# Gate parts of the modulation summed on VectorE, and a three-operation S5 scan step, in a two-layer diffusion trunk

## The chip, the core and the metric

The kernel runs on one NeuronCore of one Trainium2 chip. A core has TensorE (PE, matrix products), VectorE (DVE), ScalarE (ACT), GpSimd (POOL) and SyncE (SP), each with its own instruction queue that is worked off in order, and 16 DMA engines that bring data from HBM into the core's memory (SBUF). Products land in PSUM. The metric is the device time of one execution in microseconds, as a median over runs; a lower time is better.

## The reference

The kernel computes one inference step of two trunk layers for 128 context tokens and 128 latent tokens of width 2048. Cut to what matters here, a layer is:

```python
mod = c_silu @ w_mod[l] + b_mod[l]                      # 2048 x 6144, for the two conditions c_ctx and c
shift, scale, gate = jnp.split(mod, 3, axis=-1)
h = rms_norm(x, norm_w[l]) * (1 + scale) + shift
hg, at, s5_u, s5_g, merge = split_columns(h @ w_in[l])  # 2048 x 15872
o_hg, o_at = hgrn_branch(hg), attention(at)
u = s5_u.reshape(bsz, seq, 64, 16)                      # S5: 64 groups, 64 complex states each
s_t = abar * s_{t-1} + bbar @ u_t                       # forward, and backward over flipped tokens
y = gelu(re(c @ s) + d * s5_u)
o_s5 = y * sigmoid(y @ w_glu) * silu(s5_g)
merged = sum(sigmoid(merge_b) * (o_b @ w_br[b]) for b in (hg, at, s5))
x = x + gate * (merged @ w_out[l])
```

The modulation is a product of two vectors with a matrix of 2048 x 6144 per layer. The kernel cuts its 6144 columns into six parts of 1024: parts 0 to 3 hold shift and scale, parts 4 and 5 hold the gate, which is used only behind the product with `w_out`.

## The kernel before

Everything is in fp32. A large product goes through `gemm` (L160): its weights come in pieces of 512 KB (`raw`, L167, three buffers) through SP's queue; each piece holds two k-steps of 128 rows. Per k-step ACT rounds the weights to `wh` and DVE subtracts them to get the rest `wl` (L139), and PE makes three products (L178 to L180) for each of the two streams, in all six matmuls of 512 columns. `wh` and `wl` have four buffers each, so neither can be more than four k-steps ahead of PE.

A layer makes its products in this order: the columns of `w_in` for S5, attention and the recurrent branch, with attention, the recurrence (`hgrn_unit`) and the S5 branch worked in between; the output gates of two branches; then for each branch b the merge gates (`m0`, `m1`, `m2`) and the product with `w_br`; for the S5 branch the product with `w_glu` stands between the merge gates and `w_br`; last `w_out`.

The S5 branch is cut into four quarters per layer (`s5_quarter`, L785). A quarter forms its inputs, then runs 64 scan steps on DVE over the tile `Sb`, which holds the inputs and then the states of both directions; before, a step is four operations (L828, L830, L833, L834). When the scan is over, PE forms the output `yp` (L840, L847). `Sb`, and later `ghl` (GELU of the branch, the left side of the product with `w_glu`, L1036), lie in the one buffer of tag S16.

The modulation is made by `mod_part` (L245), one part of 1024 columns at a time. Before, PE multiplies 16 weight tiles of 128 x 1024 with the conditions as stationary side, each cut into four pieces of 256 columns that go to four column groups of the array (L274); then DVE adds the bias (L279). For parts 4 and 5, POOL stores the result in HBM, from where it is read back, spread over all partitions (`gb`), behind `w_out`. Parts (0, 4) and (0, 5) of layer 0, the first four parts of layer 1, and parts (1, 4) and (1, 5) are "side work": a generator that `gemm` advances at a set rate (`MRATE`) from the second branch's merge gates on.

What sets the order: the code gives each instruction a priority (`P_SCAN`, `P_TOP` and others; a smaller one goes first), and a scheduler that plays through a time line puts each engine's instructions into one fixed order before the program runs. A change of cost in one place can thus move instructions anywhere.

The lines that the prediction's steps touch:

```python
w = self.t(tag if isinstance(tag, str) else tag[i], "wm", (128, n * 1024))
nc.sync.dma_start(w, io["w_mod"][l, part, k][:, i * 1024:(i + n) * 1024])
...
wl = self.wp.tile([128, 512], F32R, tag="wl", name=self.nm("wl"))
...
Sb = self.t("S16", "Sb", (128, 2, 2, 8, 2, W))
...
ghl = self.t("S16", "ghl", (128, 2, 8, 256), F32R)
```

Of the kernel before, what the change touches and what calls it, by code (L numbers as in the profile page):

```python
# [15 lines left out]
ALU = mybir.AluOpType  # L16
# [12 lines left out]
MB = 2  # L29
# [19 lines left out]
P_TOP = 1_000_000  # L49
# [3 lines left out]
P_MIX = 0  # L53
# [4 lines left out]
def view(t, off, dims):  # L58
    return bass.AP(t.tensor, t.offset + off, [list(t.ap[0])] + [list(d) for d in dims])


class Builder:
    def __init__(self, tc, ctx, io):
        self.tc, self.nc, self.io = tc, tc.nc, io
        self.seq = 0
        pool = lambda name, bufs, **kw: ctx.enter_context(tc.tile_pool(name=name, bufs=bufs, **kw))
        self.cp = pool("const", 1)
        self.wp = pool("weights", 4)
        self.sb = pool("sb", 1)
        self.bufs = dict(H8=4, Z8=2, Bl=1, CC=1, S16=1, uT=1, U2=1, ys=1, q4=2, kv=2,  # L70
                         mo=1, st=10, k2=6, k4=3, gt=4, sm=18, s5i=4, p=4, sb=1, sc=1, s5t=1)
        self.pg = pool("pg", 4, space=PSUM)
        self.pm = pool("pm", 2, space=PSUM)
        self.pb = pool("pb", 2, space=PSUM)
        self.dr = pool("scratch", 1, space=DRAM)
        self.uid = 0
# [32 lines left out]
    def ts(self, n, shape, dt=F32):  # L109
        return self.t("sm", n, shape, dt)  # L110
# [99 lines left out]
    def setup(self):  # L210
        nc, io = self.nc, self.io
        mf = self.t("ys", "masks", (128, 7, 128))
        nc.gpsimd.dma_start(mf, io["masks"])
        self.msk = self.const("msk", (128, 7, 128), U8)
        nc.vector.tensor_copy(self.msk, mf)
        self.eye32 = self.const("eye32", (128, 32), src=io["eye32"])
        self.cosT = self.const("cosT", (128, 128), src=io["rope"][0])
        self.sinT = self.const("sinT", (128, 128), src=io["rope"][1])
        self.s5d = self.const("s5d", (128, L, 8), src=io["s5_d"])
        self.gate_d = self.dr.tile([L, 2, D], F32, name="gate_d")  # L220
        self.x_d = self.dr.tile([2, T, D], F32, name="x_d")
# [20 lines left out]
        nc.vector.tensor_scalar(self.oml, self.lb, -1.0, 1.0, ALU.mult, ALU.add)  # L242


    def mod_part(self, l, part, prio, tags, plan):  # L245


# [2 lines left out]
        nc, io = self.nc, self.io  # L250
        with self.prio(prio):
            bm = self.t("mo", "bm", (128, 352))[:, 0:256]
            src = io["b_mod"][l, part]
            nc.gpsimd.dma_start(bm, bass.AP(src.tensor, src.offset, [[256, 4], [0, 32], [1, 256]]))
        kb = 0
        for bank, run, burst in plan:
            ps = None
            for k0 in range(kb, kb + run, burst):
                ws = []
                for k in range(k0, k0 + burst):  # L260
                    with self.prio(P_TOP):
                        tag, n = next(tags)
                        for i in range(0, 2, n):
                            w = self.t(tag if isinstance(tag, str) else tag[i], "wm", (128, n * 1024))
                            nc.sync.dma_start(w, io["w_mod"][l, part, k][:, i * 1024:(i + n) * 1024])
                            ws += [w[:, j * 1024:(j + 1) * 1024] for j in range(n)]
# [375 lines left out]
    def s5_params(self, l):  # L642
# [50 lines left out]

        cmul(a2r, a2i, abr, abi, abr, abi)
        cmul(acr, aci, abr, abi, cr, ci)
        sc = self.const(f"s5sc{l}", (128, 384))
        o = lambda off, ds: view(sc, off, ds)
        for qd in range(4):
            for d in range(2):
                i = qd * 2 + d  # L700
                pm = lambda c: view(c, d * 32 + qd * 8, [[1, 2], [2, 2], [4, 2]])
                for ri in range(2):
                    nc.vector.tensor_copy(o(i * 16 + ri * 8, [[4, 2], [2, 2], [1, 2]]), pm(a2r))
                    for st in range(2):
                        ts(o(128 + i * 32 + ri * 16 + st, [[8, 2], [4, 2], [2, 2]]), pm(a2i), 2.0 * ri - 1.0, None, ALU.mult)
        self.s5sc[l] = sc

    def s5_input(self, l, qd, Bl, C, Sb):
# [76 lines left out]
    def s5_quarter(self, l, hh, qh, uT, U2, ys):  # L785
# [3 lines left out]
        W = NP + 1  # L789
# [32 lines left out]
        sc = self.s5sc[l]  # L822
        with self.prio(P_SCAN):
            for i in range(NP):
                p0 = self.t("p", "p0", (128, 2, 32))
                p1 = self.t("p", "p1", (128, 2, 32))
                ds = DD + NP - 2 * i
                tt(p0.rearrange("p d (j s) -> p d j s", s=2), view(sc, qd * 32, [[16, 2], [1, 16], [0, 2]]),  # L828
                   view(Sb, i, [[ds, 2], [2 * W, 16], [W, 2]]), ALU.mult)
                tt(p1, view(sc, 128 + qd * 64, [[32, 2], [16, 2], [1, 16]]),  # L830
                   view(Sb, i + RI, [[ds, 2], [-RI, 2], [W, 16]]), ALU.mult)
                cur = view(Sb, i + 1, [[ds - 2, 2], [W, 32]])
                tt(p0, p0, p1, ALU.add)  # L833
                tt(cur, cur, p0, ALU.add)  # L834
        with self.prio(P_S5):
            yp = self.psb("yp", (128, 2, 2, 2, NP))
            for k in range(2):
# [371 lines left out]
```

## Time and profile before

| | us |
|---|---|
| median of 3 runs | 2330.3 (2329.36 to 2330.72) |
| the profiled execution, its own time | 2331.88 |
| its span, first to last instruction | 2330.1 |
| PE busy in the span | 2257.9 (97%) |
| DVE busy | 1798.2 (77%) |
| ACT busy | 1180.8 (51%) |
| POOL busy | 133.9 (6%) |
| mean granted TensorE clock | 0.994 of full speed |

Busy time is the union of an engine's instructions. PE, PEld (PE's weight loads), DVE, ACT and POOL are the engines; SPq is SyncE's queue of DMA issues. "L139" is line 139 of the kernel before. The chain of work that ended last is followed back from the last instruction, at each step to what released it. A name such as `wl<-raw,wh` tells what an instruction writes and reads, without the numbers of the buffers.

### The profile page before, as it was taken

To read this page: it belongs to the slowest core of one execution; us is meant where nothing else is said; L and a number is where in the kernel's file an instruction comes from. 1 tells how busy PE (TensorE), PEld (TensorE's weight loads), DVE (VectorE), ACT (ScalarE), POOL (GpSimd) and SP (SyncE) were. 2 spreads that over 40 slices of the span, in tenths; PEclk is the share of its full clock that TensorE was granted. 3 is DMA by queue.
4 is the path that set the end of the run, shared out by engine and by line. 5 is a ranking of instruction groups with operands and counts; after the bars stand their busy time and mean duration, and the time that the engine had idled before them with its cause. 6 is when DMAs were issued, how large, how long until landed. Compare 5 with 4: busy or idle time off the path is not lost.

```text
span 2330.1 us, 38207 instructions
## 1 busy us (share of the span) xinstructions
PE 2257.9 (97%) x13192; PEld 1812.2 (78%) x13192; DVE 1798.2 (77%) x4835; ACT 1180.8 (51%) x2061; POOL 133.9 (6%) x244
## 2 busy tenths in 40 slices
PE   4999999999999999999998999999999999999997
PEld 2777877888887776887777888888878877887886
DVE  5856899799879868865565798899959968956555
ACT  3536645555554343544446565555564544454454
POOL 2000000100000100000010001000010010000000
PEclk9999999999999999999999999999999999999999
DMA  8994554355557878677874554454545677656765
GB/s 313 342 341 142 165 172 137 110 162 184 178 165 258 295 267 298 220 251 265 305 231 138 163 174 153 132 160 155 188 155 190 194 245 240 198 179 219 240 202 181
DMA packets 131490, 483.85 MB, mean 208 GB/s; under 512 B 17200, under 2 KB 17808, under 8 KB 126944
## 3 DMA queue, kind: packets, MB, share of 16 engines
q1 hardware_dynamic: 120528, 454.09, 58.2%
q0 software_dynamic: 9472, 23.97, 3.3%
q10 hardware_dynamic: 1296, 3.36, 0.4%
q8 instruction: 103, 1.69, 0.3%
q14 instruction: 91, 0.75, 0.1%
HBM read 474.36 MB, written 6.98 MB: 207 GB/s over the span
## 4 chain that ended last, share of the span: by engine, by line
PE 82%; DVE 8%; DMA 7%; issue 2%; ACT 1%; SPq 0%; POOL 0%; DVEq 0%; ACTq 0%; POOLq 0%
PE g L178 23%; PE g L180 23%; PE g L179 22%; DMA raw<-w_in 3%; DVE wl L139 3%; PE mod L274 3%; PE bu L816 3%; PE lv L432 2%; DMA raw<-w_br 2%; DMA wm<-w_mod 2%; PE tr L134 2%; PE yp L847 1%; DVE p L830 1%; DVE Sb L834 1%; ACT wh L138 1%
## 5 line engine op out<-in xcount | busy, mean ns | idle before, releaser
L138 ACT CAST wh<-raw 128x512 fp32r<-128x512 f32 x1344 | 819.4, 622 | 925.0 <-PE g L179 459.8
L139 DVE TENSOR_TENSOR wl<-raw,wh 128x512 fp32r<-128x512 f32 x1344 | 915.5, 689 | 368.5 <-ACT wh L138 319.1
L178 PE MATMUL g<-wh,hl 128*128 128x512 f32 x1984 | 785.1, 396 | 6.4 <-ACT wh L138 2.7
L179 PE MATMUL g<-wh,hh 128*128 128x512 f32 x1984 | 777.9, 392 | 0.0
L180 PE MATMUL g<-wl,hh 128*128 128x512 f32 x1984 | 700.9, 398 | 0.4 <-DVE wl L139 0.3
L178 PEld LDWEIGHTS g<-wh,hl 128*128 128x128 f32 x1984 | 373.5, 188 | 99.4 <-ACT wh L138 8.2
L179 PEld LDWEIGHTS g<-wh,hh 128*128 128x128 f32 x1984 | 373.6, 188 | 75.7 <-issue 0.2
L180 PEld LDWEIGHTS g<-wl,hh 128*128 128x128 f32 x1984 | 366.6, 189 | 82.5 <-DVE wl L139 5.8
L178 PE MATMUL g<-wh,ol 128*128 128x512 f32 x384 | 152.0, 396 | 2.5 <-ACT wh L138 2.3
L828 DVE TENSOR_TENSOR p<-s5sc,Sb 128x64 f32<-128x64 f32 x512 | 140.8, 275 | 14.9 <-ACT Sb L820 5.9
L179 PE MATMUL g<-wh,oh 128*128 128x512 f32 x384 | 149.9, 390 | 0.0
L834 DVE TENSOR_TENSOR Sb<-Sb,p 128x64 f32<-128x64 f32 x512 | 141.7, 277 | 8.9
L830 DVE TENSOR_TENSOR p<-s5sc,Sb 128x64 f32<-128x64 f32 x512 | 139.2, 272 | 0.0
L180 PE MATMUL g<-wl,oh 128*128 128x512 f32 x384 | 132.0, 393 | 0.8 <-DVE wl L139 0.8
L274 PE MATMUL mod<-wm,cs 128*32 128x256 f32 x1536 | 104.5, 404 | 26.6 <-DMA wm<-w_mod 20.1
L833 DVE TENSOR_TENSOR p<-p,p 128x64 f32<-128x64 f32 x512 | 113.6, 222 | 6.1
L274 PEld LDWEIGHTS mod<-wm,cs 128*32 128x32 f32 x1536 | 44.7, 113 | 77.1 <-DMA wm<-w_mod 24.1
L179 PE MATMUL g<-wh,mt 128*128 128x512 f32 x256 | 99.8, 390 | 0.0
L178 PE MATMUL g<-wh,mt 128*128 128x512 f32 x256 | 99.7, 389 | 0.0
L178 PEld LDWEIGHTS g<-wh,ol 128*128 128x128 f32 x384 | 72.1, 188 | 20.3 <-ACT wh L138 4.6
L180 PEld LDWEIGHTS g<-wl,oh 128*128 128x128 f32 x384 | 71.5, 188 | 17.6 <-DVE wl L139 2.4
L180 PE MATMUL g<-wl,mt 128*128 128x512 f32 x256 | 83.5, 393 | 1.7 <-DVE wl L139 1.7
(315 smaller groups left out, 2116.8 us busy)
## 6 DMA issues: line engine op xcount, KB each, us to landing
raw<-w_in SPq DMA_DIRECT2D x496, 512.0 KB, 3.8
wm<-w_mod SPq DMA_DIRECT2D x130, 512.0 KB, 7.2
raw<-w_br SPq DMA_DIRECT2D x96, 512.0 KB, 4.2
raw<-w_out SPq DMA_DIRECT2D x64, 512.0 KB, 4.3
wm<-w_mod SPq DMA_DIRECT2D x31, 1024.0 KB, 7.4
raw<-w_glu SPq DMA_DIRECT2D x16, 512.0 KB, 3.9
gb<-gate_d POOLq DMA_DIRECT2D x16, 256.0 KB, 6.0
x<-x ACTq DMA_DIRECT2D x2, 1024.0 KB, 14.0
```

Source lines behind the costliest of these rows:

```text
L134: nc.tensor.transpose(ps[:, k], src[:, k * 128:(k + 1) * 128], self.ident)
L138: self.nc.scalar.copy(hi, src)
L139: self.nc.vector.tensor_sub(lo, src, hi.bitcast(F32))
L178: nc.tensor.matmul(ps[s], lo(k)[:, sl], wh, start=(k == 0), stop=False)
L179: nc.tensor.matmul(ps[s], hi(k)[:, sl], wh, start=False, stop=False)
L180: nc.tensor.matmul(ps[s], hi(k)[:, sl], wl, start=False, stop=(k == nk - 1))
L274: nc.tensor.matmul(ps[32 * i:32 * i + 32, 0:256], self.cT[:, 2 * k:2 * k + 32], ws[k - 2 * k0][:, i * 256:i * 256 + 256], start=(k0 == kb ...
L816: nc.tensor.matmul(pps[x][:, j2, k], Bl[pr, d, ri, k, j2, :], U2[pr, j2, 2 * qh + k].rearrange("p s t -> p (s t)"), start=True, stop=True, ...
L828: tt(p0.rearrange("p d (j s) -> p d j s", s=2), view(sc, qd * 32, [[16, 2], [1, 16], [0, 2]]), view(Sb, i, [[ds, 2], [2 * W, 16], [W, 2]]) ...
L830: tt(p1, view(sc, 128 + qd * 64, [[32, 2], [16, 2], [1, 16]]), view(Sb, i + RI, [[ds, 2], [-RI, 2], [W, 16]]), ALU.mult)
L833: tt(p0, p0, p1, ALU.add)
L834: tt(cur, cur, p0, ALU.add)
```

## The change

The gate parts of both layers, (0, 4), (0, 5), (1, 4) and (1, 5), no longer go through PE's products with the condition. DVE keeps two running sums `acc` of 128 x 1024, one for each condition: for each of the 16 weight tiles and each condition one operation multiplies the tile with the condition's column (a scalar per partition) and adds it. At the end PE sums each `acc` over its partitions with a stationary tile of zeros and one column of ones, 8 matmuls of 256 columns per part. Loading is put into a function of its own, `mod_load`, whose priority, buffers and order are those of before.

In the S5 scan, the two products of a step become one of 128 elements (own part and crossed part, with a table `sc` in a new layout), then come one addition that reads the crossed half with real and imaginary part exchanged, and the update: three operations for four. Tag `p` has three buffers of twice the size; tag `va` is new; GpSimd's DMA scratch is set to 4096 bytes.

```diff
+VPARTS = {(0, 4), (0, 5), (1, 4), (1, 5)}
...
-                         mo=1, st=10, k2=6, k4=3, gt=4, sm=18, s5i=4, p=4, sb=1, sc=1, s5t=1)
+        self.bufs = dict(H8=4, Z8=2, Bl=1, CC=1, S16=1, va=2, uT=1, U2=1, ys=1, q4=2, kv=2,
+                         mo=1, st=10, k2=6, k4=3, gt=4, sm=18, s5i=4, p=3, sb=1, sc=1, s5t=1)
...
+        self.ones = self.const("ones", (128, 2, 32))
+        nc.gpsimd.memset(self.ones, 0.0)
+        for s in range(2):
+            nc.gpsimd.memset(self.ones[:, s, s:s + 1], 1.0)
...
+        if (l, part) in VPARTS:
+            acc = [self.t("va", "acc", (128, 1024)) for _ in range(2)]
+            for k0 in range(8):
+                ws = self.mod_load(l, part, k0, tags)
+                with self.prio(prio):
+                    for j, w in enumerate(ws):
+                        for s in range(2):
+                            c = self.cT[:, 4 * k0 + 2 * j + s:4 * k0 + 2 * j + s + 1]
+                            if k0 + j == 0:
+                                nc.vector.tensor_scalar(acc[s], w, c, None, ALU.mult)
+                            else:
+                                nc.vector.scalar_tensor_tensor(acc[s], w, c, acc[s], ALU.mult, ALU.add)
+                    if k0 == 7:
+                        ps = self.psm("mod", (128, 512))
+                        for i in range(4):
+                            for s in range(2):
+                                with self.prio(P_MIX if i + s else prio):
+                                    nc.tensor.matmul(ps[32 * i:32 * i + 32, 0:256], self.ones[:, s],
+                                                     acc[s][:, i * 256:i * 256 + 256], start=(s == 0), stop=(s == 1),
+                                                     tile_position=(0, 32 * i))
+                        nc.vector.tensor_add(bm, bm, ps[:, 0:256])
+                if k0 % MB == MB - 1 and k0 < 7:
+                    yield True
+            plan = ()
...
-        sc = self.const(f"s5sc{l}", (128, 384))
+        sc = self.const(f"s5sc{l}", (128, 512))
...
-                    nc.vector.tensor_copy(o(i * 16 + ri * 8, [[4, 2], [2, 2], [1, 2]]), pm(a2r))
                     for st in range(2):
-                        ts(o(128 + i * 32 + ri * 16 + st, [[8, 2], [4, 2], [2, 2]]), pm(a2i), 2.0 * ri - 1.0, None, ALU.mult)
+                        at = qd * 128 + d * 32 + ri * 16 + st
+                        nc.vector.tensor_copy(o(at, [[8, 2], [4, 2], [2, 2]]), pm(a2r))
+                        ts(o(at + 64, [[8, 2], [4, 2], [2, 2]]), pm(a2i), 1.0 - 2.0 * ri, None, ALU.mult)
...
-                p0 = self.t("p", "p0", (128, 2, 32))
-                p1 = self.t("p", "p1", (128, 2, 32))
+                p = self.t("p", "p", (128, 2, 2, 32))
                 ds = DD + NP - 2 * i
-                tt(p0.rearrange("p d (j s) -> p d j s", s=2), view(sc, qd * 32, [[16, 2], [1, 16], [0, 2]]),
-                   view(Sb, i, [[ds, 2], [2 * W, 16], [W, 2]]), ALU.mult)
-                tt(p1, view(sc, 128 + qd * 64, [[32, 2], [16, 2], [1, 16]]),
-                   view(Sb, i + RI, [[ds, 2], [-RI, 2], [W, 16]]), ALU.mult)
+                tt(p, view(sc, qd * 128, [[64, 2], [32, 2], [1, 32]]), view(Sb, i, [[0, 2], [ds, 2], [W, 32]]), ALU.mult)
                 cur = view(Sb, i + 1, [[ds - 2, 2], [W, 32]])
-                tt(p0, p0, p1, ALU.add)
-                tt(cur, cur, p0, ALU.add)
+                own = p[:, 0]
+                tt(own, own, view(p, 80, [[32, 2], [-16, 2], [1, 16]]), ALU.add)
+                tt(cur, cur, own, ALU.add)
...
-    nc = bacc.Bacc("TRN2", target_bir_lowering=False, num_devices=1)
+    nc = bacc.Bacc("TRN2", target_bir_lowering=False, num_devices=1, dynamic_dma_scratch_size=4096)
```

The scheduler's order is another one in many places. Three of them follow. The line numbers in an order are those of its own kernel: L139 before is L140 after, L178 to L180 are L179 to L181, and L828 to L834 have become L862, L865 and L866.

The first place is DVE in layer 0, ahead of the product with `w_glu`, at the end of the scan of the last quarter. `wl_10655` is the subtraction of k-step 511, `wl_10745` of 516; `Sb` holds the states, `ghl` is the left side of the product with `w_glu`, whose own weights are k-steps 528 to 543. Before:

```order
L834 TENSOR_TENSOR Sb_5242<-Sb_5242,p_1317_5766 128x2x32
L828 TENSOR_TENSOR p_1319_5772<-s5sc_341,Sb_5242 128x64
L830 TENSOR_TENSOR p_1320_5773<-s5sc_341,Sb_5242 128x64
L139 TENSOR_TENSOR wl_10655<-raw_10642,wh_10654 128x512
L833 TENSOR_TENSOR p_1319_5772<-p_1319_5772,p_1320_5773 128x64
L834 TENSOR_TENSOR Sb_5242<-Sb_5242,p_1319_5772 128x2x32
L139 TENSOR_TENSOR wl_10701<-raw_10698,wh_10700 128x512
...
L139 TENSOR_TENSOR wl_10733<-raw_10720,wh_10732 128x512
L139 TENSOR_TENSOR ghl_10904<-ys_1847,ghl_10904 128x512 x3
L139 TENSOR_TENSOR wl_10745<-raw_10742,wh_10744 128x512
```

After, where `wl_10414` and `wl_10424` are k-steps 530 and 531 and `wl_10436` is 532:

```order
L140 TENSOR_TENSOR wl_10414<-raw_10411,wh_10413 128x512
L865 TENSOR_TENSOR p_5134<-p_5134 128x64
L866 TENSOR_TENSOR Sb_4894<-Sb_4894,p_5134 128x2x32
L140 TENSOR_TENSOR wl_10424<-raw_10411,wh_10423 128x512
L862 TENSOR_TENSOR p_5138<-s5sc_345,Sb_4894 128x128
L865 TENSOR_TENSOR p_5138<-p_5138 128x64
L866 TENSOR_TENSOR Sb_4894<-Sb_4894,p_5138 128x2x32
...
L862 TENSOR_TENSOR p_5298<-s5sc_345,Sb_4894 128x128
L865 TENSOR_TENSOR p_5298<-p_5298 128x64
L866 TENSOR_TENSOR Sb_4894<-Sb_4894,p_5298 128x2x32
L140 TENSOR_TENSOR ghl_10372<-ys_1883,ghl_10372 128x512 x4
L140 TENSOR_TENSOR wl_10436<-raw_10433,wh_10435 128x512
```

The scan's last step stood behind k-step 511 and now stands behind 531; 41 steps, each of the three operations, stand between `wl_10424` and `ghl_10372` with nothing else among them. In layer 1 the same pattern holds 12 steps, behind its k-step 1203.

The second place is PE in layer 0 where the branch's output `yp` is formed. `wl_10655` is again k-step 511 of before, `wh_10700` step 512. Before:

```order
L180 MATMUL g_10454<-wl_10655,hh_1764 128x512
L847 MATMUL yp_5778<-Sb_5242,C_5236 32x128 x8
L847 MATMUL yp_5778<-Sb_5242,CC_5319 32x128 x8
L840 MATMUL yp_5778<-uT_4597,CC_5319 128x128
...
L178 MATMUL g_10668<-wh_10700,hl_554 128x512
```

After, where `wl_10359` is k-step 527 and `wh_10391` is step 528, the first of the product with `w_glu`:

```order
L181 MATMUL g_10137<-wl_10359,hh_1800 128x512
L879 MATMUL yp_5302<-Sb_4894,C_4888 32x128 x8
L879 MATMUL yp_5302<-Sb_4894,CC_4971 32x128 x8
L872 MATMUL yp_5302<-uT_4377,CC_4971 128x128
...
L179 MATMUL g_10387<-wh_10391,ghl_10372 128x512
```

`yp`, which reads the whole scan, had 16 k-steps of other products behind it; now the product with `w_glu` follows at once.

The third place is a gate part in layer 0. Before, on PE, a burst of a part stands between two k-steps of the `w_in` and `w_br` products:

```order
L180 MATMUL g_8896<-wl_9002,oh_8655 128x512
L274 MATMUL mod_9113<-wm_9111,cs 32x256 x4
L274 MATMUL mod_9113<-wm_9109,cs 32x256 x4
L274 MATMUL mod_9113<-wm_9107,cs 32x256 x4
L274 MATMUL mod_9113<-wm_9105,cs 32x256 x4
L178 MATMUL g_9015<-wh_9019,hl_554 128x512
```

After, on DVE, the sums of a part stand among the subtractions `wl`, the merge of the branches and the scan:

```order
L282 SCALAR_TENSOR_TENSOR acc_8323<-wm_8333,cs,acc_8323 128x1024
L1014 TENSOR_TENSOR merged_7079<-mg_7262,g_7266 128x512
L140 TENSOR_TENSOR wl_7394<-raw_7381,wh_7393 128x512
L282 SCALAR_TENSOR_TENSOR acc_8324<-wm_8333,cs,acc_8324 128x1024
L866 TENSOR_TENSOR Sb_2493<-Sb_2493,p_2877 128x2x32
L140 TENSOR_TENSOR wl_7406<-raw_7403,wh_7405 128x512
L140 TENSOR_TENSOR wl_7416<-raw_7403,wh_7415 128x512
L282 SCALAR_TENSOR_TENSOR acc_8323<-wm_8335,cs,acc_8323 128x1024
```

16 bursts of 32 PE records each have gone from PE's order, and 128 operations on 1024 elements have come into DVE's; the scan of a quarter that runs beside them is spread over more k-steps.

## Rows read from the trace of the kernel before

**Rows 1.** The page: busy time and share of PE; the chain's shares by engine.

```profile
PE 2257.9 (97%) x13192; PEld 1812.2 (78%) x13192; DVE 1798.2 (77%) x4835; ACT 1180.8 (51%) x2061; POOL 133.9 (6%) x244
...
PE 82%; DVE 8%; DMA 7%; issue 2%; ACT 1%; SPq 0%; POOL 0%; DVEq 0%; ACTq 0%; POOLq 0%
```

**Rows 2.** Groups by line: line, engine, operation, tiles, shapes, count | busy us, mean ns | idle

```profile
L138 ACT CAST wh<-raw 128x512 fp32r<-128x512 f32 x1344 | 819.4, 622 | 925.0 <-PE g L179 459.8
L139 DVE TENSOR_TENSOR wl<-raw,wh 128x512 fp32r<-128x512 f32 x1344 | 915.5, 689 | 368.5 <-ACT wh L138 319.1
...
L179 PE MATMUL g<-wh,hh 128*128 128x512 f32 x1984 | 777.9, 392 | 0.0
```

**Rows 3.** Timeline of PE, two product rows six apart: start us, us, instruction

```profile
803.07 0.39 PE L178 MATMUL g<-wh,hl 128*128 128x512 f32 x1
...
804.42 0.39 PE L178 MATMUL g<-wh,hl 128*128 128x512 f32 x1
```

**Rows 4.** Timeline of DVE, operations on 512 and 1024 elements in a row

```profile
231.28 0.68 DVE L139 TENSOR_TENSOR wl<-raw,wh 128x512 fp32r<-128x512 f32 x1
231.88 1.22 DVE L504 TENSOR_TENSOR q<-q,qnorm 128x1024 f32<-128x1024 f32 x1
233.01 0.69 DVE L139 TENSOR_TENSOR wl<-raw,wh 128x512 fp32r<-128x512 f32 x1
```

**Rows 5.** Timeline of PE around gate bursts of 32 and of 8 records

```profile
807.60 0.39 PE L180 MATMUL g<-wl,hh 128*128 128x512 f32 x1
807.92 1.93 PE L274 MATMUL mod<-wm,cs 128*32 128x256 f32 x32
809.78 0.50 PE L178 MATMUL g<-wh,hl 128*128 128x512 f32 x1
...
815.94 0.64 PE L274 MATMUL mod<-wm,cs 128*32 128x256 f32 x8
```

**Rows 6.** Windows, line L274 alone: PE busy (records), PEld, clock, DMA, GB/s

```profile
725.00:823.00 98.00, 16.10 (x256) 7.21 (x256) 1.00 0.86 307
1860.00:2330.00 470.00, 15.68 (x256) 7.42 (x256) 0.99 0.65 214
```

**Rows 7.** Timeline of DVE, last scan operation of layer 0

```profile
963.32 0.28 DVE L834 TENSOR_TENSOR Sb<-Sb,p 128x64 f32<-128x64 f32 x1
```

**Rows 8.** Timeline of PE, first matmul with w_glu in layer 0

```profile
992.34 0.39 PE L178 MATMUL g<-wh,ghl 128*128 128x512 f32 x1
```

**Rows 9.** Timeline of DVE, a scan step with nothing between its operations

```profile
359.74 0.28 DVE L828 TENSOR_TENSOR p<-s5sc,Sb 128x64 f32<-128x64 f32 x1
359.93 0.27 DVE L830 TENSOR_TENSOR p<-s5sc,Sb 128x64 f32<-128x64 f32 x1
360.23 0.23 DVE L833 TENSOR_TENSOR p<-p,p 128x64 f32<-128x64 f32 x1
360.49 0.28 DVE L834 TENSOR_TENSOR Sb<-Sb,p 128x64 f32<-128x64 f32 x1
360.80 0.27 DVE L828 TENSOR_TENSOR p<-s5sc,Sb 128x64 f32<-128x64 f32 x1
```

**Rows 10.** Timeline of PE at the change of layers; idle time before in brackets

```profile
1227.09 1.08 PE L134 MATMUL tr<-ident,xn 128*128 128x128 f32 x4 [6.46 <-DVE xn L322]
1230.12 1.08 PE L134 MATMUL tr<-ident,xn 128*128 128x128 f32 x4 [1.95 <-DVE xn L322]
```

**Rows 11.** Windows there: PE, PEld, DVE, ACT, POOL busy, granted clock, DMA, GB/s

```profile
1230.00:1235.00 5.00, 4.88 (x13) 3.85 (x14) 1.78 (x3) 2.36 (x6) 0.00 (x0) 0.50 0.00 0
1235.00:1240.00 5.00, 4.83 (x24) 3.80 (x22) 3.32 (x8) 2.79 (x6) 0.00 (x0) 0.93 0.00 0
```

**Rows 12.** The page, DMA issues: KB each, median us from issue to landing

```profile
wm<-w_mod SPq DMA_DIRECT2D x130, 512.0 KB, 7.2
raw<-w_br SPq DMA_DIRECT2D x96, 512.0 KB, 4.2
...
gb<-gate_d POOLq DMA_DIRECT2D x16, 256.0 KB, 6.0
```

More of the change, by code (lines that the diff above doesn't have):

```diff
@@ L69, in __init__ @@
         self.sb = pool("sb", 1)
-        self.bufs = dict(H8=4, Z8=2, Bl=1, CC=1, S16=1, uT=1, U2=1, ys=1, q4=2, kv=2,
-                         mo=1, st=10, k2=6, k4=3, gt=4, sm=18, s5i=4, p=4, sb=1, sc=1, s5t=1)
+        self.bufs = dict(H8=4, Z8=2, Bl=1, CC=1, S16=1, va=2, uT=1, U2=1, ys=1, q4=2, kv=2,
+                         mo=1, st=10, k2=6, k4=3, gt=4, sm=18, s5i=4, p=3, sb=1, sc=1, s5t=1)
         self.pg = pool("pg", 4, space=PSUM)
@@ L242, in lower_bounds, with mod_load @@
         nc.vector.tensor_scalar(self.oml, self.lb, -1.0, 1.0, ALU.mult, ALU.add)
+    def mod_load(self, l, part, k, tags):
+        ws = []
+        with self.prio(P_TOP):
+            tag, n = next(tags)
+            for i in range(0, 2, n):
+                w = self.t(tag if isinstance(tag, str) else tag[i], "wm", (128, n * 1024))
+                self.nc.sync.dma_start(w, self.io["w_mod"][l, part, k][:, i * 1024:(i + n) * 1024])
+                ws += [w[:, j * 1024:(j + 1) * 1024] for j in range(n)]
+        return ws
     def mod_part(self, l, part, prio, tags, plan):
@@ L260, in mod_part @@
                 for k in range(k0, k0 + burst):
[L261 to L266, printed above, removed]
+                    ws += self.mod_load(l, part, k, tags)
                 with self.prio(prio):
@@ L699, in s5_params @@
             for d in range(2):
-                i = qd * 2 + d
                 pm = lambda c: view(c, d * 32 + qd * 8, [[1, 2], [2, 2], [4, 2]])
                 for ri in range(2):
-                    nc.vector.tensor_copy(o(i * 16 + ri * 8, [[4, 2], [2, 2], [1, 2]]), pm(a2r))
                     for st in range(2):
-                        ts(o(128 + i * 32 + ri * 16 + st, [[8, 2], [4, 2], [2, 2]]), pm(a2i), 2.0 * ri - 1.0, None, ALU.mult)
+                        at = qd * 128 + d * 32 + ri * 16 + st
+                        nc.vector.tensor_copy(o(at, [[8, 2], [4, 2], [2, 2]]), pm(a2r))
+                        ts(o(at + 64, [[8, 2], [4, 2], [2, 2]]), pm(a2i), 1.0 - 2.0 * ri, None, ALU.mult)
         self.s5sc[l] = sc
```

## The prediction, made blind

> **What bounds the kernel now.** The shares of busy time come first: TensorE (PE) has work in 97% of the span, VectorE (DVE) in 77%, and the chain that ended last runs over PE for 82% and over DVE for 8% [rows 1]. The reader is to see there that a removed matmul is worth its full time, and that DVE counts only where PE waits for it. The groups by line show what PE does: a k-step of every product is one cast on ScalarE (ACT, 622 ns), one subtraction on DVE (689 ns) and six matmuls of 512 columns [rows 2]. Six of them take 804.42 - 803.07 = 1.35 us [rows 3], so DVE spends 0.60 us (231.28 to 231.88) [rows 4] of every 1.35 us on the subtraction, and the rest is free for the scan, the gates and now the sums. The PE row idles 3% only; I therefore add up PE's work, then look for places where the new order makes PE wait. Numbers in steps below count the `wl` rows of DVE's order, from 0; a layer has 672 of them, and the product with w_glu is steps 528 to 543 of layer 0 and 1200 to 1215 in layer 1.
>
> **What goes from PE.** A gate part is four bursts of 32 records. Around one, the next product starts 809.78 - 807.60 = 2.18 us after the last, where 0.23 would be usual, so a burst costs 1.95 us [rows 5]. Layer 0 has 256 such records and the second layer's gates have 256 [rows 6], that is 16 bursts: -31.2 us.
>
> **What comes to PE.** Each of four parts ends in 8 matmuls of 256 columns, 16 records. Four records on four column groups take (1.93 - 0.64) / 6 = 0.215 us together [rows 5]. The new order has all records of one column group in a row, and PE starts records in order, so I take 4 x 3 x 0.215 + 0.215 = 2.8 us and 0.2 for the way in: 3.0 us, 12.0 in all. If the groups overlap fully it is 4 x 0.215 + 0.23 = 1.1 (4.4 in all), if nothing overlaps 16 x 0.215 + 0.23 = 3.7 (14.7 in all). The Trainium skill (TensorEngine Tiling (Array Packing), Tiling Modes) says that different tiles load weights and multiply in parallel. By that rule alone the term would be 4.4 and the forecast 7.6 us lower; the rows of before always go round the four groups, so they show the rule but not this order.
>
> **The wait that comes.** This is the largest term, and the order shows it, not the diff. Before, the scan of the last S5 quarter of layer 0 is over 16 steps ahead of the w_glu product: its last addition is at 963.32 us and the product starts at 992.34 [rows 7, 8], 28.7 us of slack. That product needs the scan, since it reads GELU of the branch, and its tile `ghl` takes the only S16 buffer, which holds the states. The sums add 64 operations on 1024 elements to DVE before this point; a 1024-element two-input operation holds DVE for 233.01 - 231.88 = 1.13 us [rows 4], so 72 us. That is more than the slack by 44 us. The scheduler has put this in the order as 41 scan steps in one piece after the subtraction of step 531. The `wl` tiles have four buffers, so that subtraction cannot start before PE has used `wl` of step 527, which is PE's last product before the branch's output (`yp`) and w_glu. So PE has nothing to do while DVE makes 41 steps; no other work covers it.
>
> Price of a step when nothing stands between its operations: before, 360.80 - 359.74 = 1.06 us, namely 0.19 to the second product, 0.30 to the sum, 0.26 to the update, 0.31 to the next step [rows 9]. The change keeps 0.26 and 0.31 and makes of the first two one product of 128 elements. 64 more elements cost (1.13 - 0.60) / 8 = 0.07 if read in a row [rows 4]; the state is read with a stride, and the old product held DVE 0.19 where 64 elements in a row would come near 0.14 by the same rate, so up to 0.12. A step is 0.94 to 0.99; I take 0.96. Below it could be 0.87 (no growth), above 1.06 (no gain). Layer 0: 41 x 0.96 = 39.4, with 1.1 for the cast and subtraction of step 531 ahead, and 1.4 for cast and subtraction of `ghl` behind `yp` [rows 2]: +41.9 us (36.8 to 46.1). Layer 1 has the same pattern with 12 steps behind step 1203: 11.5 + 2.5 = +14.0 us (11.5 to 15.3). Queued behind the scan on DVE are `ghl` and all later `wl`; PE and then ACT wait for them.
>
> **The clock.** At the change of layers PE idled 6.46 us [rows 10]; the granted clock was then 0.50, the 1.2 GHz level, and came back to 2.4 GHz at about 1235.7 us, 8.6 us after PE began again, of which it idled 1.95 [rows 10, 11]. Half speed over 6.7 us loses 3.3. I take 3 us behind each new wait: +6 (0 to 8.6). The Trainium skill (TensorE: Matmul & The Clock Gate, Part 1) holds that the throttled state is the default and activity releases it. By that rule both restarts are at half speed; without it the forecast is 6 us lower. These rows agree with it.
>
> **DVE while the sums run.** In the four stretches in which the sums stand (steps 297-339, 378-421, 949-990, 1050-1094) the order gives DVE 174 subtractions, 120 sums, 4 first products, 22 scan steps and 22 gate products or additions: 174 x 0.60 + 120 x 1.13 + 48 x 0.6 = 269 us (0.6 for a scan step by its starts, an estimate), against 174 x 1.35 + 4 = 239 us on PE [rows 3, 4]. The excess is 30 us; the four `wl` buffers let DVE enter each stretch 5.4 us ahead, which hides at most 22. So 8 to 30; I take 15, since DVE does not enter with a full lead where gates were evacuated just before.
>
> **Costed at nothing.** The shorter scan step saves DVE time elsewhere, where PE bounds it anyway; if PE waited there it would be a small gain. The setup has 32 more copies of 8 elements; they stand behind the first products' work. `p` has three buffers of one step each, no wait. GpSimd stores the gate and fetches the next bias earlier in its order. The smaller DMA scratch could hold a GpSimd load back; the gates' `gb` loads take 6.0 us to land and stand at the end [rows 12], so at worst +6.
>
> Sum: -31.2 + 12.0 + 41.9 + 14.0 + 6 + 15 = +57.7 us. The profiled execution took 2331.9 us (span 2330.1), 1.6 above the median of the runs; I put the sum on the median: 2330.3 + 57.7 = 2388.0 us, and about 2389.6 for a profiled one.
>
> **Rivals.**
> *The new waits don't show* (faster). If DVE were far ahead of PE, or the 41 steps ran beside matmuls, there would remain -31.2 + 12.0 + 8 = -11.2: 2319 us. For it: DVE is free 23% of the span, and the step has one operation less. Against it: the order is fixed, and the four buffers forbid DVE to be more than four steps ahead. It decides from the point where both waits and DVE's excess together stay under 19 us. Chance 0.07.
> *The loads hold PE* (slower still). A gate weight's buffer is now freed by a sum on DVE, and in SyncE's queue the next products' weights stand behind that load, 6 or 7 steps ahead of their use. DVE needs 6.5 x 269 / 174 = 10.0 us for these; a gate load lands in 7.2 us and a product's in 4.2 [rows 12], 11.4 if one follows the other. 1.4 us at some 20 of the loads is +28: 2416 us. For it: the sum is tight; against: transfers overlap, and before they have about the same lead counted from PE. Chance 0.10.
> *The three-operation step is no shorter* (the change doesn't do what it says): the product takes as long as the two it replaces, 1.06 a step, 53 x 0.10 = +5: 2393 us. Chance 0.06.
>
> **Numbers.** The forecast has 0.77. Its own range is the sum of the lower ends, -31.2 + 4.4 + 36.8 + 11.5 + 0 + 8 = +29.5 (2360 us), to that of the upper, -31.2 + 14.7 + 46.1 + 15.3 + 8.6 + 30 = +83.5 (2414 us). To hold 8 in 10 I take 2354 to 2410: the upper corner needs every term at its end, and the first rival, at 2319, is left out. Slower by over 0.2% (4.7 us, what this measurement can tell from no change): 0.92; within it 0.02; faster 0.06, nearly all from the first rival.
>
> **What would show it.** PE idles about 42 us in one piece ahead of `yp` and w_glu in layer 0 and about 13 in layer 1, released by DVE's `Sb` update, with DVE busy only with scan steps; the granted clock is at half behind both. Scan steps there are 0.94 to 0.99 us apart. The sums hold DVE 1.13 us each, PE's bursts are gone from 725 to 823 us, and PE waits for `wl` in those stretches. Wrong would be: PE busy through both places, or a sum that takes a time far from 1.13 us.

## The result and the profile after

| | us | ratio to before, 95% interval |
|---|---|---|
| before, runs beside the changed kernel | 2330.5 (2329.4 to 2331.5) | |
| changed kernel | 2398.5 (2394.0 to 2401.0) | 1.029 [1.0272, 1.0307] |
| predicted | 2388.0 (2354 to 2410) | |

The changed kernel is 68 us slower; the profiled execution has a span of 2399.0 us against 2330.1. The page's busy shares and its chain answer to [rows 1]:

```profile
PE 2248.8 (94%) x12744; PEld 1801.5 (75%) x12744; DVE 1903.7 (79%) x4471; ACT 1169.9 (49%) x2059; POOL 134.7 (6%) x247
...
PE 77%; DVE 10%; DMA 9%; issue 3%; ACT 2%; SPq 0%; DVEq 0%; ACTq 0%
```

PE has 9 us less work in a span that is 69 us longer. Where the difference stands is told by PE's waits in the changed kernel (engine, line, what it waited for: us in total, times, longest):

```profile
PE yp L879 <- DVE Sb L866: 55.1, 2, 42.0
PE g L179 <- ACT wh L139: 23.3, 18, 3.5
...
PE g L181 <- DVE wl L140: 9.6, 20, 1.4
...
PE g L179 <- DVE ghl L140: 3.0, 2, 1.5
```

The first and the last line are the waits in front of w_glu. In the kernel before, neither was there, and the two in between were:

```profile
PE g L178 <- ACT wh L138: 5.0, 8, 1.5
...
PE g L180 <- DVE wl L139: 2.7, 5, 1.0
```

PE's time line shows the first wait, its 1.51 us companion, and half speed between them: a group of 16 `yp` takes 1.08 us, later 0.64.

```profile
1025.69 1.08 PE L879 MATMUL yp<-Sb,C 128*32 128x128 f32 x16 [42.04 <-DVE Sb L866]
1026.54 1.08 PE L879 MATMUL yp<-Sb,CC 128*32 128x128 f32 x16
...
1030.80 0.64 PE L879 MATMUL yp<-Sb,C 128*32 128x128 f32 x16
...
1034.83 0.50 PE L179 MATMUL g<-wh,ghl 128*128 128x512 f32 x1 [1.51 <-DVE ghl L140]
...
2173.46 1.08 PE L879 MATMUL yp<-Sb,C 128*32 128x128 f32 x16 [13.06 <-DVE Sb L866]
...
2182.22 0.50 PE L179 MATMUL g<-wh,ghl 128*128 128x512 f32 x1 [1.51 <-DVE ghl L140]
```

What DVE does meanwhile is told by two windows (length, busy us of PE, PEld, DVE, ACT, POOL, then granted clock, DMA share, GB/s) and by a piece of its time line:

```profile
983.60:1025.70 42.10, 0.06 (x3) 0.01 (x3) 37.81 (x127) 1.24 (x3) 0.00 (x0) 0.53 0.07 25
1025.70:1031.00 5.30, 5.30 (x76) 3.93 (x80) 0.00 (x0) 0.00 (x0) 1.47 (x4) 0.53 0.04 9
```
```profile
999.96 0.39 DVE L862 TENSOR_TENSOR p<-s5sc,Sb 128x128 f32<-128x128 f32 x1
1000.38 0.23 DVE L865 TENSOR_TENSOR p<-p 128x64 f32<-128x64 f32 x1
1000.64 0.27 DVE L866 TENSOR_TENSOR Sb<-Sb,p 128x64 f32<-128x64 f32 x1
1000.95 0.38 DVE L862 TENSOR_TENSOR p<-s5sc,Sb 128x128 f32<-128x128 f32 x1
```

The window holds 127 DVE records, and 41 steps are 123 of them; the DMA engines rest too. A step takes 1000.95 - 999.96 = 0.99 us, against 1.06 in [rows 9]. Where the sums stand, each holds DVE for 641.40 - 640.21 = 1.19 us:

```profile
639.60 0.69 DVE L140 TENSOR_TENSOR wl<-raw,wh 128x512 fp32r<-128x512 f32 x1
640.21 1.28 DVE L282 SCALAR_TENSOR_TENSOR acc<-wm,cs,acc 128x1024 f32<-128x1024 f32 x1
641.40 0.27 DVE L866 TENSOR_TENSOR Sb<-Sb,p 128x64 f32<-128x64 f32 x1
```

The added matmuls push the next product back to 728.64 - 727.30 = 1.34 us after the one ahead of them, where 0.23 is usual; so 1.11 us, though the four records of a column group stand in a row in PE's order. Four of the 16 records have started by 727.8 and eight by 728.0, so the groups ran beside each other:

```profile
727.30 0.39 PE L180 MATMUL g<-wh,hh 128*128 128x512 f32 x1
727.62 1.09 PE L288 MATMUL mod<-acc,ones 128*32 128x256 f32 x16
728.64 0.74 PE L181 MATMUL g<-wl,hh 128*128 128x512 f32 x2
```

### The profile page after: what moved, and what is told of

It reads as the page before. It is cut to its first block, busy times and chain, and to the rows that moved or that the text cites. A ratio compares the mean times of both kernels' runs of the same rounds, so it can differ in the third digit from the quotient of the medians.

```text
span 2399.0 us, 36966 instructions
## 1 busy us (share of the span) xinstructions
PE 2248.8 (94%) x12744; PEld 1801.5 (75%) x12744; DVE 1903.7 (79%) x4471; ACT 1169.9 (49%) x2059; POOL 134.7 (6%) x247
## 4 chain that ended last, share of the span: by engine, by line
PE 77%; DVE 10%; DMA 9%; issue 3%; ACT 2%; SPq 0%; DVEq 0%; ACTq 0%
PE g L179 21%; PE g L181 21%; PE g L180 21%; DMA raw<-w_in 4%; DVE wl L140 3%; PE bu L851 2%; PE lv L467 2%; PE mod L309 2%; DMA raw<-w_br 2%; PE tr L135 2%; DMA wm<-w_mod 1%; PE yp L879 1%; DVE p L862 1%; DVE acc L282 1%; DMA raw<-w_out 1%
## 5 line engine op out<-in xcount | busy, mean ns | idle before, releaser
L139 ACT CAST wh<-raw 128x512 fp32r<-128x512 f32 x1344 | 812.0, 621 | 941.1 <-PE g L180 430.2
L140 DVE TENSOR_TENSOR wl<-raw,wh 128x512 fp32r<-128x512 f32 x1344 | 907.2, 686 | 324.2 <-ACT wh L139 263.5
L179 PE MATMUL g<-wh,hl 128*128 128x512 f32 x1984 | 784.7, 396 | 14.1 <-ACT wh L139 11.8
L180 PE MATMUL g<-wh,hh 128*128 128x512 f32 x1984 | 778.6, 392 | 0.0
L181 PE MATMUL g<-wl,hh 128*128 128x512 f32 x1984 | 698.1, 400 | 7.8 <-DVE wl L140 7.0
L179 PEld LDWEIGHTS g<-wh,hl 128*128 128x128 f32 x1984 | 373.8, 188 | 105.2 <-ACT wh L139 17.7
L181 PEld LDWEIGHTS g<-wl,hh 128*128 128x128 f32 x1984 | 364.4, 189 | 96.7 <-DVE wl L140 21.8
L180 PEld LDWEIGHTS g<-wh,hh 128*128 128x128 f32 x1984 | 374.1, 189 | 77.2
L862 DVE TENSOR_TENSOR p<-s5sc,Sb 128x128 f32<-128x128 f32 x512 | 201.2, 393 | 15.6 <-ACT Sb L855 7.1
L179 PE MATMUL g<-wh,ol 128*128 128x512 f32 x384 | 152.7, 398 | 10.0 <-ACT wh L139 9.9
L282 DVE SCALAR_TENSOR_TENSOR acc<-wm,cs,acc 128x1024 f32<-128x1024 f32 x120 | 152.3, 1280 | 0.5 <-DMA wm<-w_mod 0.4
L180 PE MATMUL g<-wh,oh 128*128 128x512 f32 x384 | 150.0, 391 | 0.0
L866 DVE TENSOR_TENSOR Sb<-Sb,p 128x64 f32<-128x64 f32 x512 | 140.6, 275 | 9.1
L181 PE MATMUL g<-wl,oh 128*128 128x512 f32 x384 | 127.7, 392 | 1.0 <-DVE wl L140 0.9
L865 DVE TENSOR_TENSOR p<-p 128x64 f32<-128x64 f32 x512 | 113.4, 222 | 8.4
L179 PE MATMUL g<-wh,mt 128*128 128x512 f32 x256 | 100.2, 391 | 1.7 <-ACT wh L139 1.7
L180 PE MATMUL g<-wh,mt 128*128 128x512 f32 x256 | 99.9, 390 | 0.0
L179 PEld LDWEIGHTS g<-wh,ol 128*128 128x128 f32 x384 | 72.1, 188 | 30.9 <-ACT wh L139 15.0
L309 PE MATMUL mod<-wm,cs 128*32 128x256 f32 x1024 | 73.0, 415 | 23.4 <-DMA wm<-w_mod 16.8
L181 PE MATMUL g<-wl,mt 128*128 128x512 f32 x256 | 83.6, 394 | 1.8 <-DVE wl L140 1.7
L181 PEld LDWEIGHTS g<-wl,oh 128*128 128x128 f32 x384 | 71.6, 188 | 17.7 <-DVE wl L140 2.5
L180 PEld LDWEIGHTS g<-wh,oh 128*128 128x128 f32 x384 | 72.2, 188 | 14.3
```

The source lines that it names most:

```text
L139: self.nc.scalar.copy(hi, src)
L140: self.nc.vector.tensor_sub(lo, src, hi.bitcast(F32))
L179: nc.tensor.matmul(ps[s], lo(k)[:, sl], wh, start=(k == 0), stop=False)
L180: nc.tensor.matmul(ps[s], hi(k)[:, sl], wh, start=False, stop=False)
L181: nc.tensor.matmul(ps[s], hi(k)[:, sl], wl, start=False, stop=(k == nk - 1))
L282: nc.vector.scalar_tensor_tensor(acc[s], w, c, acc[s], ALU.mult, ALU.add)
```

## The experiments

The theory: the sums take DVE's time from the scan, so that its last steps stand alone in front of w_glu, and what does not fit beside the products delays these. The rivals: the scan step itself, the loads, and a gain that a better place would bring. Times are medians, with the ratio to before on the same chip; before took 2330.5 to 2333.6 us on the chips used, so runs on different chips can't be compared closer than about 3 us. Where a PE time is split up, it is the time from each PE record's start to the next, summed over the trace by what the record writes and reads.

**The parts apart.** `scan_only`:

```diff
-VPARTS = {(0, 4), (0, 5), (1, 4), (1, 5)}
+VPARTS = set()
```

> Only the three-operation scan step; all gate parts stay on PE as before. Theory (the loss is the place that the gate sums take from the scan on DVE): in the order the last scan quarters end 38 and 73 subtractions ahead of w_glu, so no scan stands on the path: 2330 us (2326 to 2334), no gap of PE over 7 us. Rival (the new step or its table is itself slow where it runs beside matmuls): 2336 us or more, with PE waiting for DVE in the stretches with scans.

Measured: 2338.8 us, 1.003 [1.0016, 1.0044]. A miss by 5 us, and on the rival's side, though PE shows no new gap of more than 1.3 us in layer 1. Is it the smaller DMA scratch? `scratch`:

```diff
-    nc = bacc.Bacc("TRN2", target_bir_lowering=False, num_devices=1)
+    nc = bacc.Bacc("TRN2", target_bir_lowering=False, num_devices=1, dynamic_dma_scratch_size=4096)
```

> The kernel before with GpSimd's DMA scratch set to 4096 bytes, nothing else; the order of every engine is that of before. It tells apart where the 6 us of the scan-only run come from. Theory (they come from the new order, in which the scan pieces stand at other places beside PE's S5 preparation): the ratio to before is 1.000 within 0.0015, 2332 us. Rival (the smaller scratch holds GpSimd's loads back): 2337 to 2340 us.

Measured: 2332.5 us, 1.0003 [0.9991, 1.0014]. The scratch costs nothing that this shows; the 6 us belong to the new scan and the order it brings; scan-only changes little else.

`gates_only`, with the scan lines of before, their table `sc` and the four buffers of `p`:

```diff
-                tt(p, view(sc, qd * 128, [[64, 2], [32, 2], [1, 32]]), view(Sb, i, [[0, 2], [ds, 2], [W, 32]]), ALU.mult)
+                tt(p0.rearrange("p d (j s) -> p d j s", s=2), view(sc, qd * 32, [[16, 2], [1, 16], [0, 2]]),
+                   view(Sb, i, [[ds, 2], [2 * W, 16], [W, 2]]), ALU.mult)
...
```

> Only the gate sums; the scan step keeps its four operations. Theory: the order now puts 59 and 18 serial steps ahead of w_glu instead of 41 and 12; at 1.06 us for 0.99 that is 62.5 + 19.1 in place of 42.0 + 13.1 of waiting, so 2398.5 + 26.5 = 2425 us (2417 to 2433). Rival (the loss comes from the sums' own work on DVE and the loads behind them, the waits only stand where it shows): within 6 us of 2398.5.

Measured: 2430.0 us, 1.0426 [1.0404, 1.0447]. PE's time line has the two waits as worked out (62.5 and 19.1):

```profile
1055.90 1.08 PE L882 MATMUL yp<-Sb,C 128*32 128x128 f32 x16 [62.68 <-DVE Sb L869]
...
2197.46 1.08 PE L882 MATMUL yp<-Sb,C 128*32 128x128 f32 x16 [19.44 <-DVE Sb L869]
```

So the wait is, within 2 us, the number of steps in the order times the step. In the changed kernel the three-operation step saves some 30 us of the damage that the sums do.

`gates_l0` and `gates_l1`, sums in one layer each:

```diff
-VPARTS = {(0, 4), (0, 5), (1, 4), (1, 5)}
+VPARTS = {(0, 4), (0, 5)}
```

> The three-operation scan, and sums only for the gates of the first layer; those of the second stay on PE. Theory: layer 0 has the same order as in the changed kernel (41 steps in one piece), layer 1 that of the scan alone. The trace of the changed kernel stands 46 us behind that of before at the end of layer 0, so 2330.5 + 46 = 2376 us (2371 to 2381), PE gap 42 us in layer 0 and none in layer 1. Rival (the layers do not add up: what layer 0 loses is partly given back or doubled in layer 1, by clock or loads): outside 2368 to 2384.

Measured: 2384.7 us, 1.0229 [1.0211, 1.0247], with one wait of 42.08 us. It is 46 us above scan-only, as the theory has it for layer 0; I had put it on the time before and so missed the 6 us of the scan. That lands on the rival's side of my bound, but not for the rival's reason.

```diff
-VPARTS = {(0, 4), (0, 5), (1, 4), (1, 5)}
+VPARTS = {(1, 4), (1, 5)}
```

> The three-operation scan, and sums only for the gates of the second layer. The order of layer 0 is that of the scan-only kernel, that of layer 1 that of the changed kernel (12 steps in one piece ahead of w_glu). Theory (the layers add up, since each layer's loss is made in its own order): the changed kernel less the layer-0 run, 2398.5 - 2384.7 = 13.8, on the scan-only 2338.8: 2352.6 us (2347 to 2358), one PE gap of 13 us. Rival (layer 1 loses more or less when it starts undisturbed): outside that range.

Measured: 2358.7 us, 1.0117 [1.0091, 1.0143], just outside. The median says neither. In the traces the second layer is 15.6 us longer than in scan-only, and 15.5 in the changed kernel; the rest of the difference in the profiled executions, 6.6 us, stands in layer 0, whose order is the same in both. The layers add up as far as this can tell: two executions of one order can differ by more. `before` and `scratch`, whose orders are the same, reach the change of layers at 1227.09 and 1238.14 us, 11 us apart.

**DVE or the loads?** `half_cols`, sums over half the columns:

```diff
-                                nc.vector.scalar_tensor_tensor(acc[s], w, c, acc[s], ALU.mult, ALU.add)
+                                nc.vector.scalar_tensor_tensor(acc[s][:, 0:512], w[:, 0:512], c, acc[s][:, 0:512], ALU.mult, ALU.add)
...
```

> The changed kernel with all loads, but the sums are made over 512 of the 1024 columns (half of the gate parts is left out). An addition then costs about 0.65 us for 1.20. In the order there is one piece of 15 scan steps ahead of w_glu in layer 0 and none over 4 in layer 1. Theory (DVE's time for the sums makes both the waits and the excess): the scan-only time 2338.8 - 30.7 + 4.5 for PE's share, + 15 x 0.99 + 2.6 for the one wait, + 2 for the clock, excess 0 (DVE then needs 202 us where PE needs 239): 2332 us (2325 to 2342), one PE gap of 15 to 18 us. Rival (the excess in the gate stretches is made by the weight loads and what stands behind them in SyncE's queue, which are unchanged): 26 us more, 2358 us or above, with ACT waiting for raw in those stretches.

Measured: 2336.9 us, 1.002 [1.001, 1.003]; 15.56 us of wait. PE's waits beside it, 7.2 and 5.9 us for `wh` and `wl`, are nearly those of scan-only (6.2 and 5.2), with all loads made:

```profile
PE yp L879 <- DVE Sb L866: 15.6, 1, 15.6
...
PE g L179 <- ACT wh L139: 7.2, 9, 2.0
...
PE g L181 <- DVE wl L140: 5.9, 10, 1.0
```

`after_one_load` is the counterpart, all sums and an eighth of the gate loads:

```diff
-                ws = self.mod_load(l, part, k0, tags)
+                ws = self.mod_load(l, part, k0, tags) if k0 == 0 else ws
```

> The changed kernel with all sums, but each gate part loads only its first two of 16 weight tiles, and all 32 operations read these (the rest of the gate weights is left out). The order keeps the 41 and 12 scan steps and the sums' places within a step or two. Theory (DVE's time makes the excess in the gate stretches): 2398 us (2390 to 2403), PE still waits for wl and wh there. Rival (the gate loads stand in front of the products' weights on full DMA engines, and these make the excess): some 24 us less, 2375 us (2368 to 2382).

Measured: 2392.5 us, 1.0262 [1.0233, 1.0292]: 6 us go with the loads. In the four stretches with sums that the prediction names, PE's records of the products take 15.5 us longer than in scan-only in the changed kernel, 11.4 without most of the loads and 6.7 with half of the sums. So the excess there is mostly DVE's time; `half_cols` also has another order, so the split is not exact. PE's waits for `wh` in these stretches, 11.6 us in the changed kernel, fall to 1.2 in this run and 2.3 in `half_cols`: they need both the sums and the loads.

**Another place.** `late` puts all sums behind the scan, and advances the side work at another rate (`MRATE`):

```diff
-            acc = [self.t("va", "acc", (128, 1024)) for _ in range(2)]
+            acc = [self.t("uT", "acc", (128, 1024)), self.t("CC", "acc", (128, 1536))[:, 0:1024]]
...
-                parts = [(l, 4), (l, 5)] + [(l + 1, q) for q in range(4)]
+                parts = [(l + 1, q) for q in range(4)] + [(l, 4), (l, 5)]
...
```

> All four gate parts as sums, but placed behind the scan: the two sums use the buffers that the last S5 quarter holds until its output is formed, layer 0 first makes the next layer's four parts on PE, and in layer 1 the side work starts behind the S5 branch. In the order no scan step stands in a piece of more than four, and the sums stand from steps 490 to 610 and 1150 to 1290. Theory (order): the saving on PE comes through, -31.2 + 4.4 and some 4 to 12 of DVE's excess where 17 to 24 sums meet 32 subtractions: 2312 us (2304 to 2322), no PE gap over 7 us. Rival (sums cost DVE and loads what they cost wherever they stand): 2345 us or more, PE waiting for wl and wh through the stretches with sums. Between the two, 2322 to 2345, the excess is the larger share than I think.

Measured: 2345.3 us, 1.0059 [1.0042, 1.0076]. The waits in front of w_glu are gone, and with them most of the loss, but there is no gain: the rival's bound. Against scan-only the bursts save 30.7 us on PE as they should, the added matmuls cost 5.2, and 32 us are lost elsewhere. The longest gap, 5.85 us at 2193.16, stands in this window of `late`:

```profile
2186.00:2193.00 7.00, 1.31 (x6) 0.75 (x4) 3.14 (x3) 0.51 (x1) 0.00 (x0) 0.97 1.00 326
```

DMA share 1.00 at 326 GB/s, while PE works 1.31 us, ACT 0.51 and DVE 3.14 of the 7: here the gate weights and the products' weights fill the DMA engines. ACT waits for a load, and PE for ACT:

```profile
2192.49 1.14 ACT L139 CAST wh<-raw 128x512 fp32r<-128x512 f32 x2 [6.76 <-DMA raw<-w_br]
```
```profile
2193.16 0.79 PE L179 MATMUL g<-wh,ol 128*128 128x512 f32 x1 [5.85 <-ACT wh L139]
```

`late_one_load`, with the edit of `after_one_load`:

> The run with four late parts, again with only the first two of 16 weight tiles of each gate part loaded. The order is that of the late run within a few steps. That run lost some 32 us against the sum of its saved bursts and added matmuls, and its longest gap stands in a window in which the DMA engines were busy all the time. Theory now (behind the scan the gate loads and the products' loads together fill the DMA engines): 2338.8 - 30.7 + 5.2 = 2313 us and 0 to 8 of excess: 2317 us (2312 to 2325). Rival (DVE's sums stand before the products' own work in DVE's order): 2345 us (2338 to 2350), as in the late run.

Measured: 2328.2 us, 0.998 [0.9968, 0.9991]. Half of the 32 us go with the loads; the other half stays. Neither theory alone. For sums at this place the run is also a bound: with seven eighths of the gate weights not even loaded, the change gains 0.2%. Both runs also move the next layer's parts ahead of the gates, and there is no run with that order and no sums; how much of the other half is the sums' own time is not shown.

`late_one`, the kernel before with its old scan, and one part per layer on DVE:

```diff
+VPARTS = {(0, 5), (1, 5)}
...
+                    for p in [(l, 4)] + [(l + 1, q) for q in range(3)]:
+                        yield from part(*p)
+                    for pair in zip(part(l, 5), part(l + 1, 3)):
+                        yield from pair
...
```

> Scan with four operations, and one gate part per layer as sums, the second, placed behind the scan in the buffers of the last S5 quarter; in layer 0 it alternates with the last part of the next layer on PE. Theory (DVE has room for 32 sums behind the scan, not for 64 in a bunch): 8 bursts x 1.92 = -15.4, + 2.6 for the added matmuls, + 4 to 12 of excess: 2327 us (2322 to 2334). Rival (any sum in these stretches makes PE wait for its full excess, half of what the run with four late parts lost, 2 x 8 us): 2336 us or more.

Measured: 2336.1 us, 1.0018 [1.001, 1.0027]: the rival. Even 32 sums, placed where DVE had been free for some 20 us in each 32 k-steps, go with a loss that is larger than the 15.4 us that PE saves. This run moves the next layer's parts as well, so it is not shown that the sums alone make the loss.

`paced`, old scan, three parts, one buffer for their loads:

```diff
+                tags = itertools.cycle([("Bl", 2)])
...
```

> Scan with four operations; three gate parts as sums behind the scan, (0, 5), (1, 4) and (1, 5), fed through one buffer of 1 MB, so that a load of 7.7 us and four sums of 4.8 us follow each other: 32 sums per 74 steps at most, DVE 0.6 + 0.52 us per step for PE's 1.35. Theory (the excess of the late run is bunching): 12 bursts = -23.0, + 3.9 for the added matmuls, + 3 to 12 of excess: 2321 us (2315 to 2330), faster than both kernels. Rival (a waiting gate load at the head of SyncE's queue now holds the next products' weights back): 2335 us or more, ACT waiting for raw behind steps 512 to 586 and 1152 to 1290.

Measured: 2362.5 us, 1.013 [1.0115, 1.0144]. Much slower, and at least in part in a way that neither had: a sum now waits on its own load at the head of DVE's queue, and the products' `ol` stands behind it. DVE and then PE:

```profile
2158.92 2.48 DVE L287 SCALAR_TENSOR_TENSOR acc<-wm,cs,acc 128x1024 f32<-128x1024 f32 x2 [5.05 <-DMA wm<-w_mod]
2161.32 0.68 DVE L140 TENSOR_TENSOR ol<-o,oh 128x512 fp32r<-128x512 f32 x1
```
```profile
2162.06 0.80 PE L179 MATMUL g<-wh,ol 128*128 128x512 f32 x1 [7.52 <-DVE ol L140]
```

Such waits for `ol` make 12.0 us in six pieces; the rest of the loss is not taken apart here.

`split`, the changed kernel with the second part of each layer late:

```diff
-            acc = [self.t("va", "acc", (128, 1024)) for _ in range(2)]
+            acc = ([self.t("va", "acc", (128, 1024)) for _ in range(2)] if part == 4 else
+                   [self.t("uT", "acc", (128, 1024)), self.t("CC", "acc", (128, 1536))[:, 0:1024]])
```

> The changed kernel, but the second gate part of each layer takes its two sums in the buffers that the last S5 quarter holds until its output is formed; the first part stays where it was. In the order the last piece of scan steps ahead of w_glu is 22 steps in layer 0 (41 in the changed kernel) and none over 4 in layer 1 (12). Theory (the wait is steps times 0.99, the excess stays with the sums): 2398.5 - 19 x 0.99 - 13.1 - 1.5, and some 5 less for the clock: 2360 us (2351 to 2369), PE gap 22 to 24 us in layer 0, none over 8 us in layer 1. Rival (the excess is made by two parts following each other closely): below 2348 us, near the run with four late parts.

Measured: 2435.0 us, 1.0443 [1.0409, 1.0477]. The wait came as expected, 22.94 us, and layer 1 is 10 us shorter than in the changed kernel. But in layer 0 the part's sums, held back until the scan ended, kept the weight buffers that the next layer's parts need, and those were worked off in one heap:

```profile
977.44 1.08 PE L880 MATMUL yp<-Sb,C 128*32 128x128 f32 x16 [22.94 <-DVE Sb L867]
...
1033.40 1.06 PE L289 MATMUL mod<-acc,ones 128*32 128x256 f32 x2 [18.17 <-DVE acc L283]
...
1050.41 3.64 PE L310 MATMUL mod<-wm,cs 128*32 128x256 f32 x32 [6.72 <-DMA wm<-w_mod]
```

PE waits 54.5 us for `wm` in this trace, against 16.8 in the changed kernel. I had looked only at the scan in the order, not at what queued behind the held part. No version with the full work beats the kernel before.

## Why the prediction was right, point by point

The direction, the place and the size came out as forecast; 10.5 us were missing. The terms were off by more than that, in both directions; that the sum came so close is in part luck. The measured column is the changed kernel against scan-only, from the starts of PE's records, one execution of each; the last row is scan-only against before, by the medians.

| term | predicted | measured |
|---|---|---|
| 16 bursts less | -31.2 | -31.2 |
| added matmuls | +12.0 | +4.1 to 4.5 |
| wait in layer 0 | +41.9 | 42.04 + 1.51 = +43.6 |
| wait in layer 1 | +14.0 | 13.06 + 1.51 = +14.6 |
| half clock behind them | +6 | 2.3 + 1.9 = +4.2 |
| excess in the gate stretches | +15 | +15.5 |
| the products outside the stretches | no term | +11.1 |
| shorter scan step | 0 | +6.3 (2338.8 - 2332.5) |

With 4.1 for the added matmuls, the rows but the last make 61.9 of the 62.2 us between the two spans. The rows for the clock are, of before, where the `yp` of a quarter takes 970.46 - 965.14 = 5.32 us at full speed, and of the changed kernel two windows at half speed:

```profile
965.14 0.65 PE L847 MATMUL yp<-Sb,C 128*32 128x128 f32 x16
...
970.46 0.49 PE L178 MATMUL g<-wh,hl 128*128 128x512 f32 x1
```
```profile
1095.50:1098.90 3.40, 3.40 (x12) 2.19 (x15) 3.10 (x7) 2.40 (x5) 0.00 (x0) 0.50 0.45 155
1747.50:1750.90 3.40, 3.40 (x12) 2.71 (x11) 3.40 (x8) 2.58 (x6) 0.00 (x0) 0.50 0.52 178
```

- *The waits.* Right, by counting steps in the order and pricing one: 41 x 0.99 + 1.1 = 41.7 for the 42.04. The 0.96 was a little low. It held again for 59, 18, 15 and 22 steps.
- *The added matmuls.* Mis-sized by 8 us: I let records of one column group, standing in a row, hold the others back. They did not, and 1.11 us per part is the lower end that I had given. The Trainium skill (TensorEngine Tiling (Array Packing), Tiling Modes), by which the term would be 4.4, agrees with this trace.
- *The clock.* Right in kind, too large by 2 us. The granted clock is 0.53 in the first wait and in the 5.3 us behind it, so at the 1.2 GHz level for most of both, and the 13.06 us wait ends at half speed too. The Trainium skill (TensorE: Matmul & The Clock Gate, Part 1) has the throttled state as the default, and this trace agrees. Behind the two waits the `yp` of a quarter takes 1034.83 - 1.51 - 1025.69 = 7.63 and 2182.22 - 1.51 - 2173.46 = 7.25 us for the 5.32. What I did not count is that the clock can fall behind short waits as well: the two windows at 0.50 stand behind waits for `wh` of 2.04 and 1.79 us, and half speed over 3.40 us loses some 1.7 in each. It does not fall behind every such wait; there is no such stretch behind the longest one, of 3.5 us.
- *The excess.* Right in the four stretches for which it was worked out: 15.5 us, and 17.8 where the same orders stand in `gates_l0` and `gates_l1`. Its sign was half right: PE idles 17.1 us there, 5.5 of it for `wl`, as I said, and 11.6 for `wh` (in scan-only 5.6, nearly all in front of the bursts). A sum holds DVE 1.19 us instead of 1.13, which is 120 x 0.06 = 7 us more work than in my 30.
- *The products outside the stretches.* Here a term was missing. Of the 11.1 us, 5.9 stand in steps 432 to 463, just behind the second stretch; PE's longest wait for `wh`, 3.5 us, is there. `gates_l0` repeats them (5.4), and leaving out most of the loads or half of the sums hardly changes them (4.8 and 4.5), so they seem to come with the new order of layer 0; what makes them stays open. The other 5 us are within what two executions of one order differ. The rival with the loads, at 0.10 and 28 us, was thus a small part of what happened: 6 us by `after_one_load`.
- *Costed at nothing.* Wrong for the scan step: alone it is 6.3 us slower. The traces put this in layer 1, in many places of 1 to 3 us beside the S5 preparation: from the change of layers to the end they have 1110.6 us in scan-only and 1110.0 in `gates_l0`, which has the same order there, against 1103.0 in before and 1101.2 in `scratch`. `scratch` excludes the DMA scratch. Whether the step or only its new places beside PE make it stays open.
- The two rivals that would have made it faster, or the step no shorter, are out: PE idled at both places, and the step fell from 1.06 to 0.99.

## What to carry to other kernels

Here PE, the engine that bounds the kernel, was busy 97% of the span and DVE was free a quarter of it, and still none of the ways tried here of moving the gate work to DVE paid: a serial chain and the products' own work stood behind the moved work in DVE's queue. So look first at what is queued behind the moved work: in a queue that is worked off in order, its time turns into waits. Count in the order, not in the diff, how many steps of a serial chain stand alone between two products, multiply by the step, and the wait is known, in these runs within 2 us. Check as well which buffers the moved work holds and who needs them next.

## What the runs showed of the hardware

- Matmuls of the same column group in a row did not hold back the other groups: 16 records of 256 columns on four groups delayed PE by 1.11 us, and eight of them had started within 0.4 us.
- Behind two waits of PE, of 2.04 and 1.79 us, the granted clock was 0.50 for 3.40 us of work; behind one of 3.5 us it was not.
- A scalar_tensor_tensor of 1024 fp32 elements holds DVE 1.19 us, 0.06 more than the two-input operation of [rows 4].
- The DMA engines were busy all of a window at 326 GB/s; in that state weights came so late that PE idled 5.85 us.
- Two executions with the same order of every engine differed by 11 us over layer 0 (`before` and `scratch`).
